# One order of block products for all groups, and work at the edges of the mixer stage moved

## The chip, the core and the metric

The kernel runs on one core of one Trainium2 chip. The core has five engines with a queue each: TensorE (PE, matrix products, which accumulate in PSUM), VectorE (DVE) and ScalarE (ACT, element-wise work), GpSimd (POOL) and SyncE (SP), the last two used here mostly to issue transfers by DMA. The metric is the device time of one execution in microseconds (us); lower is better.

## The reference

One layer of a decoder on x (2048 x 1024, float32): an RMS norm, one projection to 3584 columns, two mixers side by side (a gated short convolution over 512 columns, and a recurrent block, RG-LRU, over 1024), a projection back, and an MLP of width 4096.

```python
h = rmsnorm(x, norm_mix_g[l])
u = jnp.einsum('bsd,dc->bsc', h, w_in[l])
gate_b, gate_c, v, x_r, g = jnp.split(u, split_pts, axis=-1)
y_conv = gate_b * causal_dwconv(gate_c * v, conv_w[l])
xr = causal_dwconv(x_r, rnn_conv_w[l]) + rnn_conv_b[l]
y_rnn = rg_lru(xr, w_a[l], b_a[l], w_x[l], b_x[l], lru_lambda[l])
y_rnn = y_rnn * jax.nn.gelu(g)
y = jnp.concatenate([rmsnorm(y_conv, g_norm_conv[l]),
                     rmsnorm(y_rnn, g_norm_rnn[l])], axis=-1)
x = x + jnp.einsum('bsc,cd->bsd', y, w_out[l])
h = rmsnorm(x, norm_mlp_g[l])
z = jnp.square(jax.nn.relu(jnp.einsum('bsd,df->bsf', h, w_mlp_in[l])))
x = x + jnp.einsum('bsf,fd->bsd', z, w_mlp_out[l])
return rmsnorm(x, final_norm_g)
```

In `rg_lru` two small block-diagonal products give two gates (sigmoids), and a scan along the sequence follows.

## The kernel before

**Tiling.** The 2048 rows go through in two halves of 1024; each half is two blocks of 512 (TB), and a block is four row tiles of 128. Every float32 operand is split into a high part (a cast, ACT, L172) and a low part (a subtraction, DVE, L173), and each product is three matmuls: high by high, high by low, low by high (`passes`, L228). A matmul is 128 x 128 by 128 x 512.

**The projection's groups.** The columns of W_in are cut into seven groups (L43 to L45), taken in the order SEQUENCE = 0, 4, 1, 5, 2, 6, 3. Groups 0 to 3 hold 256 columns of x_r ("x0" to "x3") and 256 of g ("g0" to "g3"); 4 and 5 hold those of C ("c0", "c1") and of v ("v0", "v1"); 6 holds those of B ("b0", "b1"). Each LRU group ends in two units (`Lru`, L476): `conv` (four DVE operations, then the split into xr_hi and xr_lo), `gate` (12 small matmuls into two PSUM tiles "psri", then four sigmoids), `scan`, and `out`. The last three trail behind the products of the following groups.

**First half, `mixers_plain` (L676).** The products are plain: per set of 256 columns two blocks (`both`, L687) of 48 matmuls (`col_products`, L243). Because the factor of the RMS norm multiplies a row of x, it is applied when a PSUM tile is drained, as R: the factors of 512 rows are put on a diagonal (`diagonal`, L355) and spread over all partitions by a product with ones (`spread`, L361), then copied from PSUM by ACT (L400). At the start the first block of x0 is computed in the tile `start_x` (L436), then g0's first block, the first spread, x0's second block, the second spread, g0's second block (L715 to L751). `around` (L693) puts the gate of the group before between the two blocks of the next group, and its scan behind them. On PE, the order here comes from the compiler's own scheduling, as on the other engines.

**Second half, `mixers_blocks` (L938).** Here each group is done by Strassen's scheme in the form of Winograd: seven products of 24 matmuls in place of eight (`block_product`, L830). They share three accumulators: x takes products 1, 6, 7 and 4, y takes 2, w takes 5 and 3; a `drain` after each product reads the sum as it stands. The LRU groups ran in ORDER_LRU = 1 2 6 5 3 7 4 and the others in ORDER = 1 2 6 5 7 3 4. In an LRU group the drain of 5 is an ACT copy of w (L869), that of 7 a DVE sum over x (L871), that of 3 completes x_r (L873) and starts `conv` of the first unit, that of 4 is a pair of Gelus (L880, L881). `step` (L948) runs the gates and scans of the group behind, at products given by STEPS and STEPS2; for group 3 `between` (L988) runs them inside the following product with W_out. On PE the order in this part is the order of the code.

**Weights kept for the second half.** The split weights of products 1, 2 and 4 ("ws") and the sums of quarters for 5, 6, 7 and 3 ("wk", `keep_sums`, L667, four DVE operations in place on the raw tiles) are written to DRAM on POOL's queue. Tiles for weights come from a pool of 15 (`wp`); PSUM tiles from a pool of 4 (`psp`), each of two banks. The writes for units 0 and 1 (x0 and g0) are held back in `held` and issued after `seen`, a POOL copy that reads R (L730 to L733).

**Behind the mixers.** `stats` (L626) sums squares per row by matmuls with ones into two PSUM tiles "sps" one after the other, which DVE reads (L636). Then come the products with W_out: first the convolution's part (`w_out_conv`), then the recurrent part (`OutRows`), whose first four steps `multiply(0, t, w)` each open a PSUM tile "po" and hold it until the row tile is finished (`end`).

Of the kernel before, what the change touches and what calls it, by code (L numbers as in the profile page):

```python
# [14 lines left out]
P = 128  # L15
# [23 lines left out]
ORDER = (1, 2, 6, 5, 7, 3, 4)  # L39
ORDER_LRU = (1, 2, 6, 5, 3, 7, 4)  # L40
STEPS = {1: 0, 6: 1, 5: 2, 7: 3, 3: 4}
# [21 lines left out]
def block_kernel(  # L63
# [36 lines left out]

    queued = [None]

    def temp(name, shape=(P, 2, TB), dt=F32):
# [30 lines left out]
    def spill_r(nm, t, queue):  # L134
        d = dp.tile(list(t.shape), F32, name="d_" + nm)
        queue.dma_start(d, t.bitcast(F32))
        return d
# [65 lines left out]
    def note_split(u, rs, pairs):  # L203
        n = units[u][3]
        if n is not None:
            rawkept.setdefault(n, []).extend(rs)
            f = u % 2
            for half, i in ((0, 1), (1, 2)) if f == 0 else ((1, 4),):
                if u < 2:
                    held.append((n, i, pairs[half]))  # L210
                else:
                    kept[n, i] = [spill_r("ws", t, nc.gpsimd) for t in pairs[half]]
        splits[u] = tuple(zip(*pairs))
# [17 lines left out]
    def mm_cols(ps, w, h, j, ks):  # L231
        for k in ks:
            pl = passes(w, h(k))
            for i, (ws, hs) in enumerate(pl):
                nc.tensor.matmul(  # L235
                    ps[:, j, :],
# [3 lines left out]
                    stop=k == KD - 1 and i == len(pl) - 1,  # L240
                )

    def col_products(nm, w, h):  # L243
        ps = psum("ps_" + nm[0])
        for ks in (range(4), range(4, KD)):
            for j in range(2):
                mm_cols(ps, w, h, j, ks)
        return ps
# [111 lines left out]

    def spread(rs, n, diag=None):  # L361
        if diag is None:
            diag = diagonal(rs, n)
        ps = psum("bc", (P, n * P))
        nc.tensor.matmul(ps, ones, diag.rearrange("p n q -> p (n q)"), start=True, stop=True)
        return ps
# [5 lines left out]
    class Rows:  # L372
# [25 lines left out]

        def spread(self, bc):
            nc.scalar.copy(bc, spread(self.rs, NT))  # L400

# [274 lines left out]
    def mixers_plain(h):  # L676
# [16 lines left out]
        def around(nm, drain, steps):  # L693
            w = both(nm, drain, (0,))
            if steps:
                late.gate()
            both(nm, drain, (1,), w)
            if steps:
                late.scan()

        for n in SEQUENCE:
            if n < 4:
# [12 lines left out]
                if pr == 0:  # L715
# [5 lines left out]
                    firsts[0].factors()  # L721
                    firsts[0].spread(R[:, 0, :])
                    drain_x(0, start_x)
                    drain_g(0, pss[0])
                    for k in range(4):
                        firsts[1].part(k)
                    both("x0", lambda blk, ps: pss.append(ps), (1,), w_first)
                    firsts[1].factors()
                    firsts[1].spread(R[:, 1, :])
                    seen = nc.gpsimd.tensor_copy(warm, R[:, 1, 0:1]).ins  # L730
                    with tc.issue_after(seen):
                        for m, i, pair in held:
                            kept[m, i] = [spill_r("ws", t, nc.gpsimd) for t in pair]  # L733
                    drain_x(1, pss[1])
                else:
                    around("x%d" % pr, drain_x, late)
# [11 lines left out]
                last = latest[0]  # L748
                if pr == 3:
                    rA = stats(mix.acc["A"], 512, "A")  # L750
                both("g%d" % pr, drain_g, (1,), wg)  # L751
                if pr == 3:
                    ysA = conv_operands(fetched)
                u0.gate(gw)
                u0.scan()
                late = Late(mix, u0, u1, g, gw)
                with tc.issue_after(last):
                    keep_sums(n)
                continue
# [178 lines left out]
    def mixers_blocks(H, more):  # L938
        G = [InLru(n) for n in range(4)] + [InConv(n) for n in (4, 5)] + [InGate(6)]
        order = [ORDER_LRU if n < 4 else ORDER for n in range(NG)]  # L940
        two = SEQUENCE[:2]
        seq = [(n, i) for n in two for i in order[n][:2]]
        seq += [(n, i) for n in two for i in order[n][2:]]
        seq += [(n, i) for n in SEQUENCE[2:] for i in order[n]]
        behind = {b: a for a, b in zip(SEQUENCE, SEQUENCE[1:]) if a < 4}
# [16 lines left out]
        for n in range(-FETCHW, len(seq)):  # L962
# [20 lines left out]
            if s == 3 and i == 6:  # L983
                rA = stats(mix.acc["A"], 512, "A")
            if s == 3 and i == 3:
                fetched = [fetch_y(mix.ys["A"], q, 0) for q in range(2)]
# [326 lines left out]
    for b in range(0, NB, 2):  # L1313
# [8 lines left out]
        with tc.manual_schedule(engines={nc.tensor.engine}):  # L1322
# [29 lines left out]
            w_out_conv(b + 1, ysA[2:], ws, rA, during)  # L1352
            rB = stats(mix.acc["B"], D, "B")
            for n in range(2):
                w = take("oB%d" % n, 1)
                rows[0].fetch(2 + n)
                if n:
                    rows[0].split(1)
                for t in range(NT):
                    rows[0].multiply(n, t, w)  # L1360
            for n in (2, 3):
# [164 lines left out]
        if more:  # L1526
# [3 lines left out]
            def finish_operands(n):  # L1530
                if n == 0:
                    ops.put(ops.begin(3), r1[2:])
                if n == 1:
                    ops.put(ops.begin(7), r1[:2])
                if n == 2:
# [50 lines left out]
```

## Time and profile before

| what | us |
|---|---|
| median of 3 runs | 2194.44 |
| lowest and highest | 2192.04, 2194.78 |
| the profiled execution | 2197.27 |
| its span, first to last instruction | 2195.4 |
| PE busy in it | 2140.6 |
| DVE busy | 1481.7 |
| ACT busy | 967.6 |

A line of the profile's groups reads: line of the kernel, engine, operation, output <- inputs, shapes, count, then busy time, mean ns of one, and the idle time of the engine just before them with what ended it. In the list of waits a row is: the instruction that waited <- what released it, then total us, times, longest. In a time line a row is: start, length, engine, line, operation, output <- inputs, shapes, count, and in brackets the idle time before it. PE's clock is shown as a share of full speed; the profile's matmuls overlap, and their ends are modelled.

### The profile page before, as it was taken

How to read it: one execution, taken by the hardware profiler on the slowest of the kernel's cores; microseconds unless marked ns; L12 is line 12 of the kernel's file. 1: busy time of each engine (PE TensorE's matmuls, PEld its weight loads, DVE VectorE, ACT ScalarE, POOL GpSimd, SP SyncE). 2: the span in 40 equal slices, each digit the busy share in tenths (PEclk: the TensorE clock that was granted, in tenths of full speed). 3: DMA queues.
4: the chain of work that ended last, by engine and by line, in shares of the span. 5: the costliest groups of instructions: out<-in, count | busy, mean ns of one | idle time of the engine just before them, and what ended most of it. 6: DMA issues, size and time to landing. Idle time of an engine off the chain costs nothing. (4 is left out here: it accounts for less than half of the span.)

```text
span 2195.4 us, 25100 instructions
## 1 busy us (share of the span) xinstructions
PE 2140.6 (98%) x9488; PEld 1752.8 (80%) x9488; DVE 1481.7 (67%) x1726; ACT 967.6 (44%) x1219; POOL 183.3 (8%) x335
## 2 busy tenths in 40 slices
PE   9999998999999999999999999989999999999998
PEld 7788886888888878888887777778878888888886
DVE  5877767669787876577746566694787565654456
ACT  6726437345333234453526356473533333433333
POOL 0211110000111100000021130100000000000000
PEclk9999999999999999999999999999999999999999
DMA  6946745342887789699573473754234444876431
GB/s 231 345 152 231 268 166 198 134 147 78 304 295 264 291 319 405 257 400 328 202 252 95 177 262 112 278 170 168 77 127 181 152 164 153 321 290 233 164 143 77
DMA packets 180904, 472.51 MB, mean 215 GB/s; under 512 B 15664, under 2 KB 62768, under 8 KB 179760
## 3 DMA queue, kind: packets, MB, share of 16 engines
q1 hardware_dynamic: 141104, 328.30, 41.7%
q0 software_dynamic: 36800, 133.19, 16.0%
q10 hardware_dynamic: 2880, 9.44, 1.1%
q8 instruction: 74, 1.21, 0.2%
q14 instruction: 46, 0.38, 0.1%
HBM read 308.33 MB, written 162.53 MB: 214 GB/s over the span
## 5 line engine op out<-in xcount | busy, mean ns | idle before, releaser
L847 PE MATMUL up<-H,w_hi 128*128 128x512 f32 x1792 | 552.6, 390 | 4.4 <-DVE snap L1054 3.4
L173 DVE TENSOR_TENSOR w_lo<-w,w_hi 128x1024 fp32r<-128x1024 f32 x208 | 253.2, 1222 | 270.1 <-issue 164.8
L847 PEld LDWEIGHTS up<-H,w_hi 128*128 128x128 f32 x1792 | 335.6, 188 | 75.1 <-ACT H L172 4.2
L1148 PE MATMUL dn<-w_lo,z_hi 128*128 128x512 f32 x896 | 349.6, 390 | 3.1 <-DVE w_lo L173 3.1
L1148 PE MATMUL dn<-w_hi,z_hi 128*128 128x512 f32 x896 | 349.9, 391 | 1.6 <-DVE x L1524 1.6
L1148 PE MATMUL dn<-w_hi,z_lo 128*128 128x512 f32 x896 | 349.2, 390 | 0.0
L847 PE MATMUL up<-H,w_lo 128*128 128x512 f32 x896 | 348.6, 389 | 0.0
L172 ACT CAST z_hi<-z 128x1024 fp32r<-128x1024 f32 x112 | 118.0, 1053 | 263.7 <-PE dn L1148 246.5
L172 ACT CAST w_hi<-w 128x1024 fp32r<-128x1024 f32 x208 | 215.9, 1048 | 31.3 <-DVE w L1027 15.4
L847 PE MATMUL in<-H,wr 128*128 128x512 f32 x888 | 206.9, 393 | 12.3 <-DVE g L871 7.7
L847 PEld LDWEIGHTS in<-H,wr 128*128 128x128 f32 x888 | 167.0, 189 | 51.1 <-DVE g L871 9.3
L1148 PEld LDWEIGHTS dn<-w_lo,z_hi 128*128 128x128 f32 x896 | 168.6, 188 | 39.0 <-DVE w_lo L173 3.9
L1148 PEld LDWEIGHTS dn<-w_hi,z_hi 128*128 128x128 f32 x896 | 168.5, 188 | 37.8 <-DVE x L1524 2.4
L1148 PEld LDWEIGHTS dn<-w_hi,z_lo 128*128 128x128 f32 x896 | 168.6, 188 | 35.1
L847 PEld LDWEIGHTS up<-H,w_lo 128*128 128x128 f32 x896 | 168.2, 188 | 35.1
L173 DVE TENSOR_TENSOR z_lo<-z,z_hi 128x1024 fp32r<-128x1024 f32 x112 | 136.6, 1220 | 22.7 <-ACT z_hi L172 19.9
L1041 ACT COPY snap<-up 128x1024 f32<-128x1024 f32 x48 | 48.7, 1014 | 184.5 <-PE up L847 181.0
L254 PE MATMUL po<-w_hi,y_hi 128*128 128x512 f32 x384 | 121.8, 399 | 5.7 <-ACT gi L518 4.6
L254 PE MATMUL po<-w_hi,y_lo 128*128 128x512 f32 x384 | 119.6, 393 | 1.9 <-DVE y_lo L648 1.8
L254 PE MATMUL po<-w_lo,y_hi 128*128 128x512 f32 x384 | 120.0, 394 | 0.1
L173 DVE TENSOR_TENSOR w_lo<-raw,w_hi 128x1024 fp32r<-128x1024 f32 (+1 forms) x62 | 73.4, 1186 | 63.1 <-issue 15.0
L172 ACT CAST w_hi<-raw 128x1024 fp32r<-128x1024 f32 (+1 forms) x62 | 62.9, 1019 | 116.4 <-PE ps_x L235 60.9
(265 smaller groups left out, 3105.8 us busy)
## 6 DMA issues: line engine op xcount, KB each, us to landing
z<-d_z SPq DMA_DIRECT2D x112, 512.0 KB, 7.5
w<-in_w_mlp_out_dram SPq DMA_DIRECT2D x80, 512.0 KB, 6.6
wr<-d_ws POOLq DMA_DIRECT2D x74, 512.0 KB, 6.1
w<-in_w_mlp_in_dram SPq DMA_DIRECT2D x64, 512.0 KB, 5.1
d_z<-snap SPq DMA_DIRECT2D x64, 512.0 KB, 3.1
w<-d_w SPq DMA_DIRECT2D x64, 512.0 KB, 4.7
d_z<-z SPq DMA_DIRECT2D x48, 512.0 KB, 2.9
d_ws<-w_hi POOLq DMA_DIRECT2D x37, 512.0 KB, 6.8
```

The source lines that it names most:

```text
L172: nc.scalar.copy(hi, src)
L173: latest[0] = V.tensor_tensor(lo, src, hi.bitcast(F32), SUB).ins
L254: nc.tensor.matmul(ps[:, half, :], ys[:, j, t * P : (t + 1) * P], ws[j][:, 0, half * 512 : (half + 1) * 512], start=first and i == 0, stop ...
L847: nc.tensor.matmul(ps[:, j, :], ws[:, k, j * P : (j + 1) * P], hs(k), start=i in (1, 2, 5) and k == 0 and n == 0, stop=k == 3 and n == len ...
L1041: nc.scalar.copy(t, ps)
L1148: nc.tensor.matmul(ps[t // 2][:, t % 2, :], zs[:, p, t * P : (t + 1) * P], ws[:, p, :], start=i in (1, 2, 5) and a == 0 and p == 0 and n == 0,
```

## The change

Four things are moved; no product is added or left out.

1. All groups of the second half run in ORDER. The operands for product 7 are prepared before those for 3. W_out's first two units are loaded at products 7 and 3 of group 3 instead of when they are used.
2. At the start, x0's second block comes ahead of the first spread, and the second spread stands halfway in g0's second block. The two spreads share one PSUM tile. `seen` reads R's first half; the kept weights of unit 2 (c0) are held as well, and `keep_sums` writes behind them.
3. The first gate and scan of group 0 move from behind g0 into `around` of c0, between its two blocks, and the second gate behind its second block. `keep_sums` of group 3 moves ahead of A's statistics.
4. B's statistics move from ahead of the recurrent part's products to behind the first three row tiles.

```diff
@@
-ORDER_LRU = (1, 2, 6, 5, 3, 7, 4)
@@ def spill_r
-        queue.dma_start(d, t.bitcast(F32))
+        spilled[0] = queue.dma_start(d, t.bitcast(F32)).ins
@@ def note_split
-                if u < 2:
+                if u < 3:
@@ def mm_cols, def col_products
-                nc.tensor.matmul(
+                mm = nc.tensor.matmul(
...
+        return mm.ins
-    def col_products(nm, w, h):
+    def col_products(nm, w, h, halfway=None):
...
-                mm_cols(ps, w, h, j, ks)
+                last = mm_cols(ps, w, h, j, ks)
+            if halfway and ks[0] == 0:
+                with tc.issue_after(last):
+                    halfway()
@@ def spread
-    def spread(rs, n, diag=None):
+    def spread(rs, n, diag=None, ps=None):
...
-        ps = psum("bc", (P, n * P))
+        if ps is None:
+            ps = psum("bc", (P, n * P))
@@ def around
             if steps:
+                if nm == "c0":
+                    late.u0.gate(late.gw)
+                    late.u0.scan()
+                else:
+                    late.gate()
+            both(nm, drain, (1,), w)
+            if nm == "c0":
                 late.gate()
-            both(nm, drain, (1,), w)
@@ first group
-                    firsts[0].spread(R[:, 0, :])
-                    drain_x(0, start_x)
-                    drain_g(0, pss[0])
-                    for k in range(4):
-                        firsts[1].part(k)
                     both("x0", lambda blk, ps: pss.append(ps), (1,), w_first)
-                    firsts[1].factors()
-                    firsts[1].spread(R[:, 1, :])
-                    seen = nc.gpsimd.tensor_copy(warm, R[:, 1, 0:1]).ins
+                    psR = psum("bc")
+                    firsts[0].spread(R[:, 0, :], psR[:, 0, :])
+                    seen = nc.gpsimd.tensor_copy(warm, R[:, 0, 0:1]).ins
...
+                    split_kept = spilled[0]
+                    drain_x(0, start_x)
+                    for k in range(4):
+                        firsts[1].part(k)
+                    firsts[1].factors()
+                    pss.append(
+                        col_products(
+                            "g0", wg, h[1], lambda: firsts[1].spread(R[:, 1, :], psR[:, 1, :])
+                        )
+                    )
                     drain_x(1, pss[1])
+                    drain_g(0, pss[0])
@@ each LRU group
                 if pr == 3:
+                    keep_sums(n)
                     rA = stats(mix.acc["A"], 512, "A")
-                both("g%d" % pr, drain_g, (1,), wg)
+                if pr:
+                    both("g%d" % pr, drain_g, (1,), wg)
+                else:
+                    drain_g(1, pss[2])
...
-                u0.gate(gw)
-                u0.scan()
+                if pr:
+                    u0.gate(gw)
+                    u0.scan()
                 late = Late(mix, u0, u1, g, gw)
-                with tc.issue_after(last):
-                    keep_sums(n)
+                if pr < 3:
+                    with tc.issue_after(last), tc.issue_after(split_kept):
+                        keep_sums(n)
@@ def mixers_blocks
-        order = [ORDER_LRU if n < 4 else ORDER for n in range(NG)]
...
+        seq = [(n, i) for n in two for i in ORDER[:2]]
+        seq += [(n, i) for n in two for i in ORDER[2:]]
+        seq += [(n, i) for n in SEQUENCE[2:] for i in ORDER]
...
+            if s == 3 and i in (7, 3):
+                load_unit(cursor[0] + (i == 3))
@@ recurrent part of W_out
-            rB = stats(mix.acc["B"], D, "B")
...
                 for t in range(NT):
+                    if n == 0 and t == 3:
+                        rB = stats(mix.acc["B"], D, "B")
                     rows[0].multiply(n, t, w)
@@ def finish_operands
                 if n == 0:
+                    ops.put(ops.begin(7), r1[:2])
+                if n == 1:
                     ops.put(ops.begin(3), r1[2:])
-                if n == 1:
-                    ops.put(ops.begin(7), r1[:2])
```

More of the change, by code (lines that the diff above doesn't have):

```diff
@@ L101, in block_kernel @@
     queued = [None]
+    spilled = [None]
     def temp(name, shape=(P, 2, TB), dt=F32):
@@ L397, in factors, with spread @@
             norm_rows(self.s2, NT, self.rs)
-        def spread(self, bc):
-            nc.scalar.copy(bc, spread(self.rs, NT))
+        def spread(self, bc, ps):
+            nc.scalar.copy(bc, spread(self.rs, NT, None, ps))
     firsts = [Rows(k, small("rs_x")) for k in range(2)]
@@ L939, in mixers_blocks @@
         G = [InLru(n) for n in range(4)] + [InConv(n) for n in (4, 5)] + [InGate(6)]
-        order = [ORDER_LRU if n < 4 else ORDER for n in range(NG)]
         two = SEQUENCE[:2]
-        seq = [(n, i) for n in two for i in order[n][:2]]
-        seq += [(n, i) for n in two for i in order[n][2:]]
-        seq += [(n, i) for n in SEQUENCE[2:] for i in order[n]]
+        seq = [(n, i) for n in two for i in ORDER[:2]]
+        seq += [(n, i) for n in two for i in ORDER[2:]]
+        seq += [(n, i) for n in SEQUENCE[2:] for i in ORDER]
         behind = {b: a for a, b in zip(SEQUENCE, SEQUENCE[1:]) if a < 4}
```

## The prediction

> **What bounds the kernel now.** I read the page first, for the engine that is full; then the list of waits of TensorE, for what leaves it empty; then a table of stretches, for its clock after those waits; then time lines.
>
> ```profile
> span 2195.4 us, 25100 instructions
> ...
> PE 2140.6 (98%) x9488; PEld 1752.8 (80%) x9488; DVE 1481.7 (67%) x1726; ACT 967.6 (44%) x1219; POOL 183.3 (8%) x335
> ...
> L847 PE MATMUL in<-H,wr 128*128 128x512 f32 x888 | 206.9, 393 | 12.3 <-DVE g L871 7.7
> ```
>
> TensorE (PE) is the bound: 98% busy. The change removes no product, so all that it can win is waits and what follows them. The waits of PE, with total, number and longest:
>
> ```profile
> PE in L847 <- DVE g L871: 7.7, 4, 2.0
> PE sps L632 <- DVE xr L547: 5.2, 1, 5.2
> PE in L847 <- ACT g L869: 4.7, 4, 1.4
> PE po L254 <- ACT gi L518: 4.6, 2, 4.1
> ...
> PE psri L504 <- ACT xr_hi L172: 2.8, 1, 2.8
> PE psri L504 <- DVE xr_lo L173: 2.5, 3, 1.0
> PE bc L365 <- DVE diag L358: 2.0, 1, 2.0
> ```
>
> Nearly all of these lie at places that the edits touch. A wait costs more than its idle time, as the stretches show (length, then busy time and count per engine, granted clock, DMA share, GB/s):
>
> ```profile
> 1275.00:1305.00 30.00, 30.00 (x134) 24.82 (x134) 27.98 (x24) 15.49 (x16) 12.78 (x18) 1.00 0.74 251
> 30.00:37.00 7.00, 4.97 (x14) 2.98 (x13) 3.51 (x13) 6.93 (x19) 0.00 (x0) 0.76 0.71 254
> 57.50:74.20 16.70, 13.12 (x41) 8.47 (x40) 14.86 (x13) 12.90 (x12) 3.20 (x6) 0.69 0.69 259
> ...
> 362.00:371.20 9.20, 5.11 (x16) 3.75 (x15) 6.96 (x9) 8.70 (x8) 0.00 (x0) 0.81 0.58 201
> 374.50:382.50 8.00, 5.35 (x19) 2.89 (x18) 7.33 (x10) 7.65 (x8) 0.00 (x0) 1.00 0.70 241
> 1147.00:1165.00 18.00, 15.00 (x65) 11.79 (x64) 9.15 (x8) 4.31 (x5) 0.00 (x0) 1.00 0.10 30
> 1186.00:1192.00 6.00, 4.13 (x21) 2.35 (x20) 6.00 (x6) 5.26 (x5) 1.58 (x3) 1.00 0.66 212
> 1222.00:1243.00 21.00, 18.00 (x71) 14.11 (x70) 10.61 (x10) 5.33 (x5) 1.07 (x2) 0.92 0.49 163
> ...
> 1467.00:1481.00 14.00, 8.79 (x31) 7.35 (x31) 11.63 (x22) 5.71 (x9) 0.18 (x1) 0.63 0.60 193
> ```
>
> In the first, undisturbed, stretch 134 matmuls take 30 us: one per 0.22 us, though each is shown 0.39 us long (the page's row of L847). So a wait costs 0.17 us beyond its idle time. And after some waits the clock halves; what that costs is the length times what the clock lacks: 7.0 x 0.24 = 1.7 us after the first spread, 16.7 x 0.31 = 5.2 us at 57.5, 9.2 x 0.19 = 1.7 us at 362, 21 x 0.08 = 1.7 us at 1222. At 1467 the half-speed part is 14 x 0.37 x 2 = 10.4 us; between (10.4 - 5.2) / 2 = 2.6 and 8.79 / 2 = 4.4 us is lost, I take 3.7.
>
> **Part a: order 1 2 6 5 7 3 4 in the four LRU groups.** Before, 3 adds into the accumulator that 5 has just filled and ACT is copying (L869), and 4 into the one that 7 has just filled and DVE is reading (L871). The new order puts another product between each pair. Groups 4 to 6 already run in it, and the list has no wait for their copies. Removed: 7.7 + 4.7 idle, 8 x 0.17 = 1.4, and the 1.7 us of half clock: **15.5 us**. What it costs is time for the gates:
>
> ```profile
> 1155.71 1.23 DVE L873 TENSOR_TENSOR xr_in<-in,xr_in 128x1024 f32<-128x1024 f32 x1 [16.58 <-PE in L847]
> 1156.97 0.81 DVE L486 TENSOR_SCALAR xr<-xr_in,prm 128x1024 f32<-128x1024 f32 x1
> 1157.82 3.92 DVE L490 SCALAR_TENSOR_TENSOR xr<-xr_in,prm,xr 128x1024 f32<-128x1024 f32 x3
> 1161.66 1.22 DVE L871 TENSOR_TENSOR g<-in,g 128x1024 f32<-128x1024 f32 x1
> 1162.85 1.23 DVE L173 TENSOR_TENSOR xr_lo<-xr,xr_hi 128x1024 fp32r<-128x1024 f32 x1
> ```
>
> From the end of 3 to xr_lo is 1155.71 to 1164.08, 8.4 us. The first gate came three products after 3 and now comes two after: 48 matmuls x 0.22 = 10.7 us. The slack falls from about 8 to 2.3 us. DVE's drain of 7 leaves this stretch, and for group 0 the preparation of the next group's weights is now issued ahead of the convolution; but ACT may take a Gelu (1.06 us) or a table load (1.28 us) ahead of xr_hi. Bounds: nothing, to 4 gates x (2 us + 1.7 us) = 15; nearest to the slack, I take 2 us lost in all. The late second gate at 1186 stays (6.00 - 4.13 = 1.9 us idle). The exchange of the operand sums of 3 and 7 costs nothing: same instructions, still five or more products ahead of use.
>
> **Part b: the start.** PE's wait for the factors, and the two gates:
>
> ```profile
> 32.78 1.82 PE L365 MATMUL bc<-diag,ones 128*128 128x512 f32 x2 [2.03 <-DVE diag L358]
> ...
> 63.31 0.50 PE L504 MATMUL psri<-xr_hi,gate 64*128 64x512 f32 x1 [2.82 <-ACT xr_hi L172]
> 64.57 0.79 PE L504 MATMUL psri<-xr_lo,gate 64*128 64x512 f32 x1 [0.76 <-DVE xr_lo L173]
> ```
> ```profile
> 22.88 5.38 DVE L411 SCALAR_TENSOR_TENSOR h<-xT,prm,h 128x512 fp32r<-128x512 f32 x8
> ...
> 47.97 1.22 DVE L709 TENSOR_TENSOR xr_in<-ps_x,R 128x1024 f32<-128x1024 f32 x1 [7.96 <-ACT R L400]
> ...
> 69.34 1.22 DVE L173 TENSOR_TENSOR w_lo<-raw,w_hi 128x1024 fp32r<-128x1024 f32 x1
> ```
> ```profile
> 47.35 0.59 ACT L400 COPY R<-bc 128x512 f32<-128x512 f32 x1 [8.09 <-PE bc L365]
> ```
>
> x0's second block now goes ahead of the first spread. Its operand h is complete at 28.26, so it runs from the end of g0's block without a wait; the 2.0 + 0.17 + 1.7 = 3.9 us go. **A new wait takes part of it back.** PSUM has four tiles: start_x, g0's first block, x0's second, and the shared psR. g0's second block is the fifth and must wait until start_x is drained, which needs R's first half: ACT copy 0.59, DVE product 1.22 and hand-overs, as at 47.35 to 49.19: 1.9 us with 0.17 more, 2.1 us. Behind it in PE's queue stand g0, the second spread and c0. Bounds 0 (another tile freed earlier) to 3.8 (half clock after); I take 2.1, gain **1.8 us**.
>
> At 58 to 74 the gates are only half of the cause. c0's third matmul needs w_lo, written at 69.34; its tile came free late, when kept weights were on their way out:
>
> ```profile
> 54.18 0.55 POOL L136 DMA_DIRECT2D d_ws<-w_hi  x1 [4.66 <-ACT w_hi L172]
> 65.94 0.54 POOL L131 DMA_DIRECT2D d_wk<-raw  x1 [11.21 <-DVE raw L661]
> ...
> 69.72 0.53 POOL L131 DMA_DIRECT2D d_wk<-raw  x1 [0.73 <-DVE raw L664]
> ...
> 78.03 0.53 POOL L136 DMA_DIRECT2D d_ws<-w_lo  x1
> ```
>
> The held writes of x0's and g0's weights went last (to 78). Now they hang on R's first half (about 43 instead of 48), the four of c0 join them, and the group's sums go behind all ten. Ten issues of 0.53 us occupy POOL for 5.3 us; x0's four tiles come back by about 50 and c0's split can be done before c0 starts near 56. The sums' writes stay at DVE's pace, about 66; those who wait for their tiles are v0's weights, needed two blocks later, near 79. The gates then stand behind c0's first and second block, 11 us of cover each. Gain 2.8 + 0.8 + 2 x 0.17 + 5.2 = **9.1 us**; without the cover, 0.
>
> **Part c: group 3's sums earlier in block 0.** The wait of 4.1 us at 362 names ACT's sigmoid, but ACT itself stood:
>
> ```profile
> 358.05 1.05 ACT L172 CAST w_hi<-raw 128x1024 fp32r<-128x1024 f32 x1 [1.41 <-issue]
> 362.40 1.05 ACT L172 CAST w_hi<-raw 128x1024 fp32r<-128x1024 f32 x1 [3.30 <-DMA d_wk<-raw]
> ```
>
> It waited for a write of the kept sums to give back a tile. Those four sums (1.22 us each) are now traced ahead of A's statistics, where DVE had gaps. Gain 4.1 + 0.17 + 1.7 = **6.0 us**; the following waits for split operands (8.00 - 5.35 = 2.7 us idle) I leave, since PE also arrives earlier. Bounds 0 to 9.5.
>
> **Part d: B's statistics behind three products.**
>
> ```profile
> 1472.88 3.57 PE L632 MATMUL sps<-ones,xr 128*128 128x1 f32 x16 [5.21 <-DVE xr L547]
> ```
> ```profile
> 1474.79 0.16 DVE L636 TENSOR_SCALAR ys_B<-sps 128x4 f32<-128x4 f32 x1 [0.82 <-PE sps L632]
> ```
>
> Three row tiles of 12 matmuls each are 36 x 0.22 = 8.0 us of cover for a wait of 5.2: it goes, with 0.17 and 3.7 of half clock, 9.1 us. But those three hold three PSUM tiles, so both statistics and the fourth row tile go through the last one: PE waits twice for DVE's read (0.16 us). Each trip costs between 0.3 (idle DVE) and 1.5 us (one 1.22 us operation ahead); I take 0.8. So **7.5 us** gained in the second half and 1.6 lost in the first, where the list shows no such wait. The earlier loads of w_out I put at 0: none is added, four move up in SP's queue, the loads that they pass (rows of x and y) are used later than w_out, and no wait of the list hangs on them.
>
> **Sum.** 15.5 - 2 + 1.8 + 9.1 + 6.0 + 7.5 - 1.6 = 36.3 us. The profiled execution took 2197.27 us around its span of 2195.4, so it would take 2161.0; it lies 2.8 above the median of the runs, 2194.44, which gives **2158**.
>
> [...] Here a wait of 2.0 us was followed by half clock (0.76 over 30 to 37), and so was the pair of waits at 1222 to 1243 (0.92), while the like pair at 1147 to 1165 was not (1.00). [...]
>
> **Rivals.**
> 1. *The start is not followed.* In this stretch PE's order is not written by hand: before, the second gate came out after two matmuls of c0, though the code has it behind a block. If it does so again, or w_lo stays late, part b is lost: 2158 + 10.9 = 2169.
> 2. *Half clock at the statistics.* Two hand-overs among tiny matmuls could halve the clock for one stretch of 1.7 us in each half: 2162. [...] No run so far shows this place.
> 3. *Gates moderately late:* the upper bound of part a, 13 us more: 2171.
> 4. *Slower.* Product 3 comes so late that each of the eight gates of the block groups waits a whole product, 24 x 0.22 = 5.4 us, with 1.7 of half clock: 57 us lost, 2215. It decides once the chain from 3 to xr_lo is over 10.7 us; with 8.4 shown and the second gates further behind, it is remote.
>
> **Chances.** Forecast 0.60 (its own range 2148 to 2168), rivals 0.18, 0.10, 0.08, 0.04. The low end takes the uncounted waits (2.7 + 2.1 + 3.2 + gates 2 + 1.9): about 2145; the high end loses parts b and c and some gates: about 2180. A difference of 0.2%, 4.4 us, is about what a measurement can tell from none. Faster by more than that 0.93, within it 0.03, slower 0.04.
>
> **What would show it.** Right: no wait of L847 for g; c0 in one piece from near 56, gates behind its blocks; a new wait of about 2 us before g0's second block; no wait of 4 us for gi near 350; sps waiting under 1.5 us. Wrong: psri waiting for xr after the reordered groups, c0 standing for w_lo, half clock behind sps.

## The result, and the profile after

The changed kernel takes **2159.72 us** (median of 4 runs, 2158.41 to 2160.86); before took 2194.61 (4 runs beside it). The ratio is **0.984**, 95% interval 0.983 to 0.986. The prediction was 2158, and the saving that it worked out, 36.3 us, is also what the two spans differ by: 2195.4 - 2159.1 = 36.3. (The profiled execution of after took 2160.86 us for a predicted 2161.0; it lies 1.1 above its median where that of before lay 2.8 above, hence 2159.7 and not 2158.) The sum is closer than its steps were, as will be seen.

The page of the changed kernel, engines and the group of the block products (line numbers have moved: L847 is now L870, L504 is L509, L632 is L637, L254 is L258):

```profile
span 2159.1 us, 25110 instructions
...
PE 2125.7 (98%) x9488; PEld 1745.3 (81%) x9488; DVE 1481.7 (69%) x1726; ACT 966.7 (45%) x1218; POOL 184.8 (9%) x335
...
L870 PE MATMUL in<-H,wr 128*128 128x512 f32 x888 | 203.2, 390 | 0.4 <-ACT g L892 0.4
```

The same 9488 matmuls, and the idle time of the block products' group is down from 12.3 us to 0.4. The list of waits of TensorE (total us, times, longest):

```profile
PE up L870 <- DVE snap L1078: 3.4, 2, 1.7
PE po L258 <- DVE y_lo L653: 3.3, 3, 1.9
PE po L258 <- ACT w_hi L172: 3.0, 1, 3.0
PE dn L1172 <- DVE w_lo L173: 2.0, 1, 2.0
PE ps_g L235 <- DVE xr_in L720: 2.0, 1, 2.0
PE psri L509 <- DVE xr_lo L173: 1.8, 2, 1.0
...
PE sps L637 <- DVE ys_B L641: 1.0, 2, 0.7
PE po L258 <- DVE ys_B L641: 0.5, 2, 0.3
PE po L258 <- ACT gi L523: 0.5, 1, 0.5
PE in L870 <- ACT g L892: 0.4, 1, 0.4
```

Read against the list of before: the waits for g (7.7 and 4.7), for xr at the statistics (5.2), for gi (4.6), for xr_hi (2.8) and for diag (2.0) are gone or nearly so. Two are new: one for w_hi of 3.0 us, and the one of 2.0 us that the prediction expected before g0's second block. Now stretches of the same execution, for the granted clock (the column behind POOL's):

```profile
41.00:50.00 9.00, 7.01 (x22) 5.01 (x21) 3.54 (x8) 5.32 (x6) 3.83 (x8) 0.81 0.67 264
386.00:404.00 18.00, 17.49 (x79) 14.60 (x78) 8.35 (x21) 4.96 (x7) 0.00 (x0) 0.91 0.45 151
1145.00:1215.00 70.00, 68.15 (x308) 54.77 (x307) 46.98 (x42) 40.40 (x38) 14.96 (x25) 1.00 0.60 205
1384.00:1396.00 12.00, 8.79 (x24) 6.37 (x24) 6.46 (x6) 7.02 (x7) 0.00 (x0) 0.72 0.27 90
1440.00:1464.00 24.00, 23.00 (x110) 19.22 (x109) 16.90 (x32) 9.93 (x13) 0.00 (x0) 1.00 0.52 185
```

By the prediction's way of counting (length times what the clock lacks) half clock costs 9 x 0.19 = 1.7 us behind the new wait at g0, 18 x 0.09 = 1.6 us at B's statistics in the first half, 12 x 0.28 = 3.4 us behind the new wait for w_hi, and nothing in this execution at the statistics of the second half (1440 to 1464), where before had 0.63 over 14 us.

Where the time went, from the first matmul of each stage in the two traces (so an idle wait ahead of that matmul counts in the row before):

| from ... to | before | after | saved | predicted |
|---|---|---|---|---|
| start to first product of v0 | 93.2 | 82.8 | 10.4 | 1.8 + 9.1 = 10.9 |
| v0 to W_out, first half | 250.1 | 250.3 | -0.1 | 0 |
| W_out, first half | 151.1 | 146.7 | 4.4 | 6.0 - 1.6 = 4.4 |
| up and down products, first half | 621.5 | 618.5 | 3.0 | 0 |
| block products | 302.9 | 288.7 | 14.2 | 15.5 - 2 = 13.5 |
| W_out, second half | 152.1 | 147.5 | 4.5 | 7.5 |
| the rest | 624.6 | 624.6 | 0.0 | 0 |

### The profile page after: what moved, and what is told of

Same layout as the page of the kernel before. It is cut to its first block, busy times and chain, and to the rows that moved or that the text cites. A ratio compares the mean times of both kernels' runs of the same rounds, so it can differ in the third digit from the quotient of the medians.

```text
span 2159.1 us, 25110 instructions
## 1 busy us (share of the span) xinstructions
PE 2125.7 (98%) x9488; PEld 1745.3 (81%) x9488; DVE 1481.7 (69%) x1726; ACT 966.7 (45%) x1218; POOL 184.8 (9%) x335
## 5 line engine op out<-in xcount | busy, mean ns | idle before, releaser
L870 PE MATMUL up<-H,w_hi 128*128 128x512 f32 x1792 | 552.5, 390 | 4.2 <-DVE snap L1078 3.4
L870 PEld LDWEIGHTS up<-H,w_hi 128*128 128x128 f32 x1792 | 335.6, 188 | 74.8 <-ACT H L172 4.2
L870 PE MATMUL up<-H,w_lo 128*128 128x512 f32 x896 | 348.6, 389 | 0.0
L870 PE MATMUL in<-H,wr 128*128 128x512 f32 x888 | 203.2, 390 | 0.4 <-ACT g L892 0.4
L870 PEld LDWEIGHTS up<-H,w_lo 128*128 128x128 f32 x896 | 168.2, 188 | 35.2
L870 PEld LDWEIGHTS in<-H,wr 128*128 128x128 f32 x888 | 166.4, 188 | 36.0 <-ACT g L892 0.8
L258 PE MATMUL po<-w_hi,y_hi 128*128 128x512 f32 x384 | 122.1, 400 | 4.0 <-ACT w_hi L172 3.0
L258 PE MATMUL po<-w_hi,y_lo 128*128 128x512 f32 x384 | 120.0, 394 | 3.3 <-DVE y_lo L653 3.3
L258 PE MATMUL po<-w_lo,y_hi 128*128 128x512 f32 x384 | 119.9, 394 | 0.2 <-DVE w_lo L173 0.2
```

Source lines behind the costliest of these rows:

```text
L258: nc.tensor.matmul(ps[:, half, :], ys[:, j, t * P : (t + 1) * P], ws[j][:, 0, half * 512 : (half + 1) * 512], start=first and i == 0, stop ...
L870: nc.tensor.matmul(ps[:, j, :], ws[:, k, j * P : (j + 1) * P], hs(k), start=i in (1, 2, 5) and k == 0 and n == 0, stop=k == 3 and n == len ...
```

## The experiments

All times are medians beside runs of before on the same chip; ratios are to before, with the 95% interval.

**The order alone.** Before, with one order and the exchanged operand sums, and nothing else of the change.

```diff
-ORDER_LRU = (1, 2, 6, 5, 3, 7, 4)
+ORDER_LRU = (1, 2, 6, 5, 7, 3, 4)
...
                 if n == 0:
-                    ops.put(ops.begin(3), r1[2:])
-                if n == 1:
                     ops.put(ops.begin(7), r1[:2])
+                if n == 1:
+                    ops.put(ops.begin(3), r1[2:])
```

> The kernel before with the one order for all groups and the exchanged operand sums, nothing else of the change. Theory (the eight waits of the block products are for the copies of accumulators): no wait of the block products for g is left, the stage from the first block product to the first product with W_out is 14 to 17 us shorter, total about 2179. Rival (the waits move to the gates, since product 3 is one product later): psri waits for xr_lo at several gates, total 2188 or more. On the new 3.0 us wait of W_out's first product for w_hi: if the order causes it (ACT runs the last group's Gelu and xr_hi first), it is here too, 3 us or more; if the earlier loads cause it (four of 15 weight tiles taken early), it is absent here.

2180.23 us, ratio 0.994 (0.993 to 0.996). The block products take 288.0 us in place of 302.9, 14.9 less, as expected (1.7 of it is a half clock in the trace of before that isn't the order's, see part a below); in the medians the order is worth 12.4. Its list of waits has none for g, and has the new one:

```profile
PE sps L632 <- DVE xr L547: 5.8, 1, 5.8
...
PE po L254 <- ACT w_hi L172: 3.0, 1, 3.0
```

So the wait for w_hi belongs to the order, not to the moved loads, which this kernel doesn't have. The gates didn't come late: psri waits for nothing that it did not wait for before.

**The two halves of the start.** First, group 0's gates back behind g0, the earlier writes kept:

```diff
-                if nm == "c0":
-                    late.u0.gate(late.gw)
-                    late.u0.scan()
-                else:
-                    late.gate()
-            both(nm, drain, (1,), w)
-            if nm == "c0":
                 late.gate()
+            both(nm, drain, (1,), w)
...
-                if pr:
-                    u0.gate(gw)
-                    u0.scan()
+                u0.gate(gw)
+                u0.scan()
```

> The changed kernel with group 0's gates where they were (first gate and scan behind g0, second gate between c0's blocks); the writes of kept weights stay as changed. Theory (two causes at the start, gates and the tile of w_lo, each enough): the first gate comes before xr_lo, which is written at 64 us while TensorE is free at 57.5, so psri waits 4 to 6 us with half clock behind it, total 2166 to 2170. Rival (only the tile of w_lo mattered): no wait, 2160.

2170.51 us, ratio 0.990 (0.988 to 0.992). From its list of waits and its stretches:

```profile
PE psri L509 <- ACT xr_hi L172: 5.0, 1, 5.0
```
```profile
55.00:75.00 20.00, 14.50 (x57) 10.66 (x56) 17.38 (x16) 9.68 (x9) 2.52 (x5) 0.83 0.53 208
```

5.0 us idle and 20 x 0.17 = 3.4 us of half clock; v0 begins at 91.0 in place of 82.8. Then the other way round, the gates kept and the kept weights written as before:

```diff
-                if u < 3:
+                if u < 2:
...
-                    seen = nc.gpsimd.tensor_copy(warm, R[:, 0, 0:1]).ins
...
+                    seen = nc.gpsimd.tensor_copy(warm, R[:, 1, 0:1]).ins
...
-                    with tc.issue_after(last), tc.issue_after(split_kept):
+                    with tc.issue_after(last):
```

> The changed kernel with the writes of kept weights as before (units 0 and 1 held, waiting for R's second half; c0's not held; the sums not behind them); the gates stay moved. Theory (each cause enough): c0's third matmul stands for w_lo, whose tile comes back only with the writes at 66 to 78 us: c0 waits some 8 to 12 us with half clock behind it, total 2168 to 2175. Rival (only the gates mattered): c0 runs in one piece, 2160.

2177.94 us, ratio 0.993 (0.992 to 0.995), more than I had expected it to lose: v0 begins at 97.6, which is **later than in the kernel before** (93.2). VectorE's time line and the list of waits say why:

```profile
71.02 1.23 DVE L669 TENSOR_TENSOR raw<-raw 128x1024 f32<-128x1024 f32 x1
72.16 1.22 DVE L173 TENSOR_TENSOR w_lo<-raw,w_hi 128x1024 fp32r<-128x1024 f32 x1
```
```profile
PE psri L509 <- ACT gi L523: 8.0, 2, 7.8
...
PE psri L509 <- ACT xr_hi L172: 2.1, 1, 2.1
```

c0's w_lo is written at 72 to 73 us, behind the four sums, so c0 stands after two products. (That it stands there for want of a free tile, as was expected, the rows of this kernel don't show; in the changed kernel ScalarE's casts for c0 do wait for writes of kept weights, 0.96 and 0.43 us.) The compiler's order on PE fills the hole with both gates of group 0, and the second of them waits 7.8 us for the first one's PSUM tiles. Of the two parts neither pays alone: the gates without the writes lose 4.4 us at v0 against before, the writes without the gates win 2.2 (less what the spread brings), both together win 10.4.

**The first spread.** It goes halfway into x0's second block, as the second one stands in g0's:

```diff
-                    both("x0", lambda blk, ps: pss.append(ps), (1,), w_first)
                     psR = psum("bc")
-                    firsts[0].spread(R[:, 0, :], psR[:, 0, :])
+                    pss.append(
+                        col_products(
+                            "x0", w_first, h[1], lambda: firsts[0].spread(R[:, 0, :], psR[:, 0, :])
+                        )
+                    )
```

> The changed kernel with the first spreading product put halfway into x0's second block, with its own PSUM tile taken first, in place of behind that block. Theory: the new wait at group 0's second block (2.0 us at 42 us, then 3.4 us at half clock, which costs 1.7 us) comes from where the spreading product stands; both go, and with the 0.17 us before the product about 3.9 us: 2155.5 to 2157 us, and the first product ps_v at about 79 us in place of 82.8. Rival: group 0's wait is for a PSUM tile that DVE frees late whatever stands before it; then the wait comes back in the same place and the time stays at 2159 to 2160 us.

TensorE's time line in this kernel shows the spread at 39.13 and g0's second block right behind x0's, with no idle time in brackets:

```profile
39.13 1.02 PE L370 MATMUL bc<-diag,ones 128*128 128x512 f32 x2
...
42.15 0.73 PE L235 MATMUL ps_g<-h,w_hi 128*128 128x512 f32 x2
```

The wait is gone, v0 begins at 79.3 in place of 82.8, and the profiled execution took 2156.25, all as the theory said. But the median is 2162.00 (ratio 0.985, 0.982 to 0.987): the other three runs took 2161 to 2164 us. The place is shown, a gain of the whole kernel isn't; the end of this section says what may spread the runs.

**Group 3's sums back at their late place.**

```diff
-                    keep_sums(n)
                     rA = stats(mix.acc["A"], 512, "A")
...
-                if pr < 3:
-                    with tc.issue_after(last), tc.issue_after(split_kept):
-                        keep_sums(n)
+                with tc.issue_after(last), tc.issue_after(split_kept):
+                    keep_sums(n)
```

> The changed kernel with keep_sums(3) back at its late place. Theory: DVE's sums stand again ahead of y_lo in the first half's W_out stage, and the wait that the change took away there (6.0 us) comes back: 2165 to 2166 us, ps 'up' of the first half at 485 to 486 us in place of 479.8. Rival: the y_lo waits that stayed in the changed kernel (4.1 us at 358 to 365 us) take the place of it, and the sums' place is worth under 2 us: 2160 to 2162 us.

2168.19 us, ratio 0.988 (0.986 to 0.990). The up products of the first half begin at 485.6 in place of 479.8, 5.9 us later, as expected; the total is 2 us above what was. ScalarE's time line and PE's list of waits have the rows of before again, the cast that stands 3.3 us for a write of the kept sums, and the sigmoid behind it:

```profile
352.96 1.04 ACT L172 CAST w_hi<-raw 128x1024 fp32r<-128x1024 f32 x1 [3.30 <-DMA d_wk<-raw]
```
```profile
PE po L258 <- ACT gi L523: 5.2, 2, 4.6
```

**B's statistics back in front**, and then, in another kernel, behind three products but with both blocks in one PSUM tile:

```diff
-                    if n == 0 and t == 3:
-                        rB = stats(mix.acc["B"], D, "B")
...
+            rB = stats(mix.acc["B"], D, "B")
             for n in range(2):
```

> The changed kernel with B's statistics ahead of the recurrent part's products, as before. Theory (the eight microseconds of three row tiles hide the wait in the second half, the hand-overs of one PSUM tile cost 2 to 2.5 us in the first): in the second half sps waits 5 to 6 us for the sum of squares with half clock behind it, 8 us in all; in the first half 2.5 us are saved: total 2165 to 2166. Rival (the wait would have gone anyway, because earlier stalls are gone): 2158 to 2160.

2166.49 us, ratio 0.988 (0.987 to 0.990). The wait is back, and the half clock too (25 x 0.20 x 2 = 10 us at half speed; in the trace of before 2.8 of them fall into the wait itself, with the clock at 0.50 from 1470.1 to 1472.9, so I estimate that about 3.5 us are lost behind it here). The second half's W_out stage takes 155.2 us in place of 147.5:

```profile
PE sps L637 <- DVE xr L552: 5.6, 1, 5.6
```
```profile
1430.00:1455.00 25.00, 19.39 (x80) 16.15 (x79) 18.96 (x34) 10.90 (x15) 0.18 (x1) 0.80 0.57 201
```

In the first half the change is a loss, as predicted: with the statistics in front the up products begin 2.0 us earlier (477.8). But most of that is the half clock which the changed kernel's execution happened to have there. From W_out's first product to the up products it is 146.7 us in that execution, 145.3 in a second run of the same instructions (the split called earlier, below), and 144.6 here. The second kernel:

```diff
-        for blk in range(2):
-            ps = psum("sps", (P, NT))
-            for t in range(NT):
...
+        ps2 = psum("sps", (P, 2 * NT))
+        for t in range(2 * NT):
...
+        for blk in range(2):
+            ps = ps2[:, blk * NT : blk * NT + NT]
```

> The changed kernel with both blocks' statistics in one PSUM tile (one hand-over to DVE less, twice in the kernel for B; A's too). Theory: each hand-over costs PE what the list shows behind sps and ys_B (1.0 and 0.5 us in total) and, in some executions, one stretch of half clock (1.7 us); with half of them gone 0.5 to 2.5 us: 2157 to 2159 us, and at B's statistics in both halves under 0.8 us lost on PE. Rival: the wait is for DVE's queue and not for the hand-over, so the single one lasts as long as the two did: 2159 to 2160 us.

2159.54 us, ratio 0.984 (0.982 to 0.985): no difference that can be told from the changed kernel. The first half's stretch was undisturbed here, the second half's was not:

```profile
386.00:404.00 18.00, 17.59 (x86) 14.80 (x86) 7.64 (x21) 4.91 (x7) 0.00 (x0) 1.00 0.39 142
1440.00:1464.00 24.00, 22.45 (x101) 18.60 (x101) 16.66 (x33) 8.86 (x12) 0.18 (x1) 0.93 0.51 179
```

The list of its waits has a new row for the row tile that follows:

```profile
PE po L258 <- DVE rs_a L324: 2.0, 2, 1.5
```

With the statistics in a single tile the next row tile waits 1.5 us for DVE to let it go, where in the changed kernel the second half's two hand-overs took 0.7 and 0.3 us. The rival holds for the second half.

**The new wait for w_hi: four attempts.** In the changed kernel ScalarE's time line, and TensorE's row that waits, are

```profile
1384.03 1.02 ACT L903 ACTIVATE g<-in 128x1024 f32<-128x1024 f32 x1 [8.94 <-PE in L870]
1384.95 1.04 ACT L172 CAST xr_hi<-xr 128x1024 fp32r<-128x1024 f32 x1
1385.88 3.88 ACT L172 CAST w_hi<-raw 128x1024 fp32r<-128x1024 f32 x4
```
```profile
1386.98 1.22 PE L258 MATMUL po<-w_hi,y_hi 128*128 128x512 f32 x2 [2.99 <-ACT w_hi L172]
```

ScalarE is idle for 8.94 us, then does a Gelu that needs product 4, then a cast that needs the convolution, and only then W_out's weights. First, the earlier loads taken out:

```diff
-            if s == 3 and i in (7, 3):
-                load_unit(cursor[0] + (i == 3))
```

> The changed kernel without the two earlier loads of w_out (block products 7 and 3 of group 3 no longer issue them; the later place issues them as before). Theory: the 3.0 us wait of the second half's first W_out product for w_hi comes from ACT, whose queue holds the last Gelu (L903, 1384.0 us) ahead of the casts, not from the loads; the earlier loads are worth nothing and the wait stays about 3 us: 2159 to 2162 us. Rival: the earlier loads pay, and without them the raw tiles land behind the Gelu: the wait grows by 2 to 5 us and half clock follows longer, 2163 to 2167 us.

2159.23 us, ratio 0.984 (0.982 to 0.987). The wait is 3.0 us as before: the loads are worth nothing, as the prediction had it. Next the split was called earlier, behind the load at product 3 (`split_unit(cursor[0])`):

> The changed kernel with the splitting of the first w_out unit put right behind the earlier load of the second, ahead of the last Gelu of the block products in ACT's queue. Theory: the 3.0 us wait for w_hi at the second half's first W_out product and the half clock behind it (6.8 us, which costs 3.4 us) come from the Gelu standing ahead of the casts; both go: 2153 to 2155 us. Rival: another operand of that product (xr_hi or y_lo) is as late, and the wait is only renamed: 2157 to 2160 us.

2160.71 us, ratio 0.985 (0.982 to 0.987), and the wait is 3.0 us: not a test, because in this trace the instructions of every engine stand in the same order as in the changed kernel. Where the casts stand in ScalarE's queue is chosen by the scheduling, not by the place of the call. It serves as a second run of the same program, below. Then the order was forced (the casts ahead of xr_hi, the last Gelus behind the casts):

```diff
             G[s].multiply(i, H)
-            G[s].drain(i)
+            if s == 3 and i == 3:
+                split_unit(cursor[0])
+                first_cast.append(casts[-1])
+            if s == 3 and i == 4:
+                with tc.issue_after(held_cast[0]):
+                    G[s].drain(i)
+            else:
+                G[s].drain(i)
...
+                with tc.issue_after(first_cast.pop()):
+                    self.split = split_new(xr, self.new, "xr")
```

> The changed kernel with the casts of w_out's first unit put ahead of xr_hi and of the last Gelus in ACT's queue (the run with only the call moved left all queues in the same order, so it could not tell). Theory: ACT's order makes the 3.0 us wait for w_hi at the second half's first W_out product, and the half clock behind it (3.5 us) follows from the wait; both go: 2153 to 2155 us, with no row of L258 waiting for w_hi over 0.5 us. Rival 1: w_hi comes early but xr_hi, now behind two casts, makes group 3's first gate late by 2 to 3 us: 2156 to 2159 us. Rival 2: the casts stand for the transfer of the raw tiles and hold the copy of product 5's sum behind them, and the block products wait for it: 2159 to 2163 us.

2161.36 us, ratio 0.984 (0.983 to 0.986). None of the three mechanisms carries it (the copy of product 5's sum, rival 2's place, is waited for 0.9 us in place of 0.4): the wait moved to W_out's *second* unit, and 3.4 us of half clock came at the second half's statistics (24 x 0.14, the clock being 0.86 over 1440 to 1464), which in the changed kernel had none (1.00). TensorE, then ScalarE:

```profile
1382.08 0.62 PE L260 MATMUL po<-w_hi,y_hi 128*128 128x512 f32 x2
...
1388.23 1.19 PE L260 MATMUL po<-w_hi,y_hi 128*128 128x512 f32 x2 [3.26 <-ACT w_hi L172]
```
```profile
1364.97 1.05 ACT L172 CAST w_hi<-raw 128x1024 fp32r<-128x1024 f32 x1 [1.88 <-DMA raw<-in_w_out_dram]
...
1386.19 1.05 ACT L910 ACTIVATE g<-g 128x1024 f32<-128x1024 f32 x1
1387.14 1.98 ACT L172 CAST w_hi<-raw 128x1024 fp32r<-128x1024 f32 x2
```

The first unit is cast 17 us ahead of its use and W_out starts at once (1382.08), but its second unit now stands behind the same Gelus. The combined kernel (this, the first spread in x0's block, and the statistics in front in the first half alone) has the same wait, 2.9 us behind W_out's first product (1381.54 to 1384.42):

> The changed kernel with the three things together: first spread halfway in x0's second block, casts of w_out's first unit first, and B's statistics in front again in the first half alone. If the losses are separate: 3.9 us at the start, 3.0 to 6.6 at the second W_out stage, 1.1 to 2.0 at the first half's statistics, so 2147 to 2152 us. If what is won at one place comes back at the next wait: 2153 to 2157 us.

2159.21 us, ratio 0.983 (0.982 to 0.985), slower than both expected ranges: in the profiled executions it is 5.8 us ahead of the changed kernel where the up products of the first half begin (474.0 for 479.8), and 1.2 at the end of the span. Of the 4.6 in between, 3.0 went in the up and down products, which no edit touches (621.5 us in place of 618.5), and 1.7 from the block products to the end of the second W_out stage. Last, both units loaded at product 7 and both split ahead of the last Gelus:

```diff
-            if s == 3 and i in (7, 3):
-                load_unit(cursor[0] + (i == 3))
+            if s == 3 and i == 7:
+                load_unit(cursor[0])
+                load_unit(cursor[0] + 1)
...
             if s == 3 and i == 4:
-                with tc.issue_after(held_cast[0]):
+                split_unit(cursor[0] + 1)
+                with tc.issue_after(casts[-1]):
                     G[s].drain(i)
```

> As the combined kernel, with both of w_out's first units loaded at product 7 of group 3, and both split ahead of the last Gelus in ACT's queue. When only the first unit was split early, PE's wait for w_hi moved 4.6 us down the queue, to the second unit, and kept its length (3.3 us). Theory: the wait hung on both units' casts behind the Gelus, so now it goes (under 0.6 us), with the half clock behind it (3.4 us): the second half's W_out stage is 5 to 7 us shorter than in the combined kernel, which gives 2152 to 2155 us. Rival: the Gelus are now last, and the next product that needs their PSUM tile, or the first gate behind xr_hi, waits as long: 2157 to 2160 us.

2156.25 us (5 runs, 2150.57 to 2160.00), ratio 0.983 (0.982 to 0.985). No row of its list names w_hi at po any more; what it has there is

```profile
PE psri L515 <- ACT xr_hi L172: 1.3, 1, 1.3
...
PE po L260 <- DVE w_lo L173: 0.7, 1, 0.7
```
```profile
1316.00:1322.00 6.00, 5.28 (x15) 3.89 (x16) 3.96 (x4) 5.36 (x6) 0.00 (x0) 0.72 0.67 255
1398.00:1404.00 6.00, 4.79 (x18) 3.24 (x19) 5.42 (x7) 5.97 (x8) 0.00 (x0) 0.72 0.12 30
1447.00:1452.00 5.00, 5.00 (x16) 3.94 (x16) 4.66 (x16) 2.80 (x4) 0.00 (x0) 0.66 0.80 292
```

The wait and the 3.4 us behind it are gone, but the second half's W_out stage is only 2.5 us shorter than in the combined kernel, not 5 to 7: the profiled execution has three stretches of half clock in the block products and in that stage, 1.7 us each (6 x 0.28, 6 x 0.28, 5 x 0.34), behind short waits (1.5 us for w_hi in the block products, 1.3 for xr_hi, 0.3 and 0.3 at the statistics). Two of these places have their waits in the changed kernel too, without half clock (1.00 over 1300 to 1340 and over 1440 to 1464); the third has the wait for xr_hi: group 3's second gate is now reached ahead of its operand, which stands in ScalarE's queue behind the sigmoids of the first. The median lies between the two expected ranges. It is the fastest of the study, and yet its interval overlaps that of the changed kernel: no run settles a version that beats it.

**What spreads the runs.** Nine of these kernels have the same wait before g0's second block, 1.99 us in every one (TensorE is busy for 7.01 of the 9.00 us from 41 to 50). Behind it the clock fell in three (the changed kernel, sums back, statistics in front: 0.81 over that stretch) and not in six (1.00). The same stretch in two of them, first the run without the early loads, then the one with the sums back:

```profile
41.00:50.00 9.00, 7.01 (x29) 5.12 (x29) 3.55 (x8) 5.14 (x6) 3.83 (x8) 1.00 0.61 241
```
```profile
41.00:50.00 9.00, 7.01 (x22) 4.93 (x22) 3.54 (x8) 5.32 (x6) 3.82 (x8) 0.81 0.64 252
```

TensorE is busy for 7.01 us in both, but does seven matmuls less in the second. Behind the wait of 3.0 to 3.3 us for w_hi the clock fell in 12 kernels of 12, for 3.4 us of loss in most (0.72 to 0.76 over stretches of 12 to 14.3 us) and 1.7 in two (0.88 over 14 and 14.3 us). But length alone doesn't decide: a wait of 3.3 us in another place, for w_lo, left the clock at 1.00 (shown in the next section), and one of 1.3 us in the last kernel was followed by half clock (0.72 over 1398 to 1404). So the same wait paid it in one execution and not in another, and of the two waits counted here the longer paid it more often: in twelve kernels of twelve, for three of nine. An execution has some eight waits of 1 to 2 us. Only the profiled executions show where the clock fell, but the mean granted clock is known for every run: in the last kernel it was 0.998 in the run of 2150.57 us and 0.995 in that of 2160.00, which makes some 6 of the 9.4 us. Over all runs of the changed kernel and of the experiments, this clock accounts for about half of the variance between runs of one kernel (0.49, 53 runs). What makes the rest stays open.

## Why the prediction came out

**Part a, the order (15.5 - 2 = 13.5; 14.2 measured): right in its main step, near in sum by luck.** The eight waits and their half clock went (the changed kernel's clock is 1.00 from 397.5 to 1386). The 2 us for late gates did not come: the chain from product 3 to xr_lo was hidden, as 8.4 against 10.7 us said it would be. What came instead is a step that the prediction doesn't have. With 3 in the place of 7, the convolution's cast xr_hi and W_out's casts fall due on ScalarE at the end of product 4, behind a Gelu that needs that product; TensorE stands 3.0 us, then loses 3.4 at half clock (which falls into the next row of the table). The prediction looked for what is late *inside* the block products and not at the edge behind them. And the trace of before has one more stretch of half clock here (8 x 0.21 = 1.7 us), which the prediction didn't count:

```profile
1347.00:1355.00 8.00, 5.96 (x18) 4.18 (x17) 5.12 (x5) 7.04 (x7) 1.05 (x2) 0.79 0.71 279
```

It stands behind a wait of 1.5 us for w_hi that all fourteen kernels have; the last of them has half clock behind it too (0.72 over 1316 to 1322), the changed kernel has none (1.00 over 1300 to 1340). So 15.5 + 1.7 - 3.0 makes the measured 14.2: the waits were worth what was predicted, and the other two terms are one oversight and one chance.

**Part b, the start (1.8 + 9.1 = 10.9; 10.4 measured).** c0's first block runs from 57.5 us in one piece, and the gates stand behind its blocks, as foreseen. The new wait came where it was foreseen, 1.99 us for 2.1. The half clock behind it (upper bound 3.8 in the prediction) came in the profiled execution (0.81 over 41 to 50), so that the spread brought almost nothing there; in six other kernels it did not (1.00), and in three of those v0 begins near 81.7, which is 11.5 us saved. Gates and writes were rightly seen as two causes of one hole; that neither is worth much without the other (-4.4 us, and 2.2 with the spread's part in it), the runs showed.

**Part c (6.0).** The mechanism holds, down to the row: the cast that waits 3.30 us for a write. The sums' place is worth 5.9 us at the next stage and about 8 in the medians (2168.2 and 2159.7). The waits for y_lo, which the prediction left standing, are 3.3 us (1.8 in the list of before). That the first half's W_out row agrees to the tenth (4.4) is chance: in the second run of the same instructions this stage took 145.3 us, which is 5.8 saved.

**Part d (7.5 - 1.6): the cover holds, the hand-overs were priced by one number where there are two outcomes.** With the statistics in front the second half's stage is 7.7 us longer, for 7.5 predicted. Against before it shows only 4.5, because the 3.4 us behind the new wait for w_hi fall into it. But that the changed kernel's execution had no half clock at these statistics is luck. Eleven kernels, the changed one among them, have them behind three products in the second half. The stretch of 1440 to 1464, or of 1447 to 1452 in the last kernel, shows the clock at them for eight: it fell in five (0.95 with group 0's gates back, 0.93 in two, 0.86 with the casts first, 0.66 in the last) and stayed at 1.00 in three. One of the five is the second run of the same instructions (24 x 0.07 = 1.7 us):

```profile
1440.00:1464.00 24.00, 22.87 (x102) 18.91 (x101) 15.34 (x31) 9.28 (x13) 0.00 (x0) 0.93 0.45 161
```

In the first half, over 386 to 404, it fell in two of the seven kernels that this stretch shows (0.91 in the changed kernel, 0.98 with group 0's gates back; 1.00 in five). So the 1.6 us for the first half measure 0.7 without half clock and 2.1 with it, and rival 2, which the prediction gave 0.10, describes five of these eight executions in the second half. "Half clock behind sps" was one of its own signs of being wrong; it is there, for 1.7 us in three of the five and 3.4 in one.

**What was not predicted and cancels.** The up and down products of the first half took 3.0 us less. Their wait for w_lo was 3.1 us in the trace of before, with half clock behind it (9 x 0.19 = 1.7 us),

```profile
PE dn L1148 <- DVE w_lo L173: 3.1, 1, 3.1
```
```profile
810.00:819.00 9.00, 5.92 (x19) 4.45 (x18) 5.76 (x5) 2.00 (x3) 0.00 (x0) 0.81 1.01 368
```

and 2.0 in the changed kernel, with none (1.00). In the second run of the same instructions (the split called earlier) the wait was 3.3 again, without half clock:

```profile
PE dn L1174 <- DVE w_lo L173: 3.3, 1, 3.3
```
```profile
792.00:801.00 9.00, 5.68 (x25) 4.40 (x24) 6.21 (x6) 2.00 (x2) 0.00 (x0) 1.00 1.01 366
```

This stage took 619.7 us there, and from 615.8 to 621.5 in all the kernels, none of which edits it; so the 3.0 us are no gain of the change. The single sum of 36.3 is thus partly luck: 3.0 us of chance in the first half stand against 3.0 missing in the second half's W_out stage. The prediction saw half clock behind one pair of waits and not behind a like pair; the runs show both outcomes for one and the same wait (0.81 in three kernels and 1.00 in six behind the 1.99 us before g0's second block), and for the wait of 3.0 to 3.3 us for w_hi one outcome in all twelve.

## What to carry to other kernels

When a product is moved nearer to the end of a stage, look at what its drain now shares a queue with *behind* the stage: the first operands of the next one. A wait that is "removed" by giving one operand priority can go to the next operand in the same queue with its length nearly unchanged (3.0 and 3.3 us here); both have to pass the same obstacle to gain anything. And undo the parts of an edit one by one before calling any of them useless or useful: the early writes and the late gates were worth little or less than nothing alone, and together, with the moved spread, 10.4 us.

## What the hardware showed

I had expected that a wait of a given length at a given instruction costs the same in every execution. It doesn't: 1.99 us of idle TensorE cost 2.2 us (with the 0.17 that the prediction worked out), or 2.2 and 1.7 of half clock (1.00 and 0.81 over 41 to 50). Nor did the length of a wait tell whether half clock follows: 3.3 us left the clock at 1.00 in one execution (792 to 801), and 1.3 us was followed by half clock in another (0.72 over 1398 to 1404). In the traces of before and of the changed kernel half clock came in portions of 3.4 us, 1.7 us of loss each: one in seven places (as in the changed kernel, 0.50 from 45.4 to 48.7 with 0.57 over 45 to 49), two behind the wait for w_hi (0.50 from 1386.9 to 1393.5), three behind the worst waits of before (0.50 from 63.9 to 73.9 and from 1470.2 to 1480.2), and cut short only by the end of the span (0.50 from 2154.9 to 2159.1). In the kernel with the writes back 55 to 95 has 0.79, which is 40 x 0.21 = 8.4 us of loss, or five. The two runs of the same instructions differed by a portion in three places (0.81 and 1.00 over 41 to 50, 0.91 and 1.00 over 386 to 404, 1.00 and 0.93 over 1440 to 1464). The waits of 1 us and more were the same in these two, and their lengths in the lists agreed to 0.1 us for all but one (w_lo, 2.0 and 3.3 us); that is what the experiments were read by.
